# A state-space scan's start and its norm tiles: two low parts by accumulating DMA, decay sums at another place in TensorE's order, norm sums in another pool's banks

## The chip, the cores and the metric

The program runs on one core of one Trainium2 chip. The metric is the device time of one execution in microseconds (us); three executions of the kernel before took 2970.08, 2967.94 and 2969.83 us, median 2969.83. Lower is better.

## What is computed

One inference step of a two-layer streaming encoder on 1024 prompt frames and 64 frames of a running stream (1088 columns, model width 1024, fp32). Layer 0 is a Mamba-2 mixer with a SwiGLU feed-forward part, layer 1 is banded attention with a SwiGLU part; each sub-layer stands between two RMS norms. The change lies in the mixer and its scan:

```python
zxbcdt = u @ w_in                          # z, x, B, C and dt
xbc = silu(causal_conv4(xbc))              # x, B, C
dt = softplus(dt_raw + dt_bias); dA = dt * A
Acs = cumsum(dA, axis=-1)                  # within a chunk
Lm = exp(where(causal, Acs[..., :, None] - Acs[..., None, :], -inf))
CB = einsum('bcqgn,bcsgn->bcgqs', Cc, Bc)
y_diag = einsum('bcgjqs,bcsgjp->bcqgjp', CB[:, :, :, None] * Lm, xd)
chunk_states = einsum('bcsgn,bcsgjp->cbgjpn', Bc, xd * decay_to_end[..., None])
h = h * chunk_decay + chunk_states         # over chunks
y = y_diag + einsum('bcqgn,cbgjpn->bcqgjp', Cc, h_prev) * exp(Acs) + x * D
y = groupnorm(y * silu(z)) @ w_out         # RMS norm over each of 4 groups
```

## The kernel before

**Split fp32.** Every weight and activation is held as a high part h (rounded to the fp32r format) and a low part l, the rest. A product is three matmuls in one PSUM bank: h by xh (L454), h by xl (L455), l by xh (L456), over eight slices of the contraction, so a pass over one weight is 24 matmuls. `passes` (L446) issues them; after half of them and at the end it lets other work in. `Weights` loads a weight tile to a raw buffer (SP's queue, L252) and `part` (L325) splits it: ACT rounds (L340), VectorE subtracts (L341). An item that is planned with `acc` goes another way in `part`: ACT writes h (L334) and then -h in the low part's place (L335), and a DMA on POOL's queue adds the weight from memory onto it (L336). Before, only 12 parts of the feed-forward layers go that way.

**The scan's stage.** The 1088 columns are three slices (384, 384, 320), s0 to s2. First B, C and x of the first group and dt are projected slice by slice; `finish` ends that. Then the list `order` is worked off group by group; its first group is weight 1 of x and weight 0 of z, in the order x s0, x s1, z s0, z s1, z s2, x s2. An x or z pass takes one of two banks of pool pmm (tile mm) and is evicted by VectorE (L721). x goes through the convolution (L759 ACT, L761 VectorE), B and C too.

**The decay tables.** `table_task` makes dt (softplus by a polynomial, L688) and dt A (L691) on VectorE. Then on TensorE: the cumulative sums (acsp, L694), the chunk sums (lastp, L699) and the transposed table (acT, L707). ACT copies acT (row, L709), SP stores it (L710), and each `ssd_task` loads its tables MT and ea from there (L845, L848). VectorE subtracts (L854), ACT takes the exponent (L855), VectorE multiplies by CB (L878).

**A scan step** (`ssd_task`, one for each of 16 x tiles and 3 slices): transpose of x (xtp, L866), times dt (xd, L876, VectorE), times decay (xe, L877, POOL), chunk states (sp, L885), the running state (hn, L895 and L898, VectorE). For two steps at a time `ssd_out` makes yp (L816) and yo (L826), each in a bank of pool pyy, evicted by VectorE (L830, L832). The last tile of a group (every fourth) also makes the group norm's sums: `rstd` transposes them on TensorE (nst, L487), VectorE reduces (L498) and takes the root (L499 to L511); `build_y` later broadcasts the result (nbp, L517).

**PSUM.** Eight banks: pmm has 2, pax 2 (xtp, sp, bnp, cbp, acsp, lastp, nst, nbp by `ax`), pyy 4 (yp, yo, acT, and early mmp and dtp). bnp (L785) and cbp (L791) are the transpose of B and the product of C and B. A tile waits until what stood in its bank has been read.

**What sets the order.** TensorE's order is written by hand. A `Stream` keeps an estimated time, tasks are generators that yield (cost, delay, condition), and `pump` steps those that are due wherever `passes` or `unit` lets it. TB_V is the delay of `table_task` between dt A and acsp, in that estimate. The other engines' queues are put in order by a scheduler with priorities, and each works its queue in order.

Of the kernel before, what the change touches and what calls it, by code (L numbers as in the profile page):

```python
# [8 lines left out]
F32 = mybir.dt.float32  # L9
# [7 lines left out]
P = 128  # L17
# [27 lines left out]
AT_W1, AT_W2 = 6.0, 2.5  # L45
SSD_GAP, SSD_D = 4.4, 8.0
ST_W, ST_RB = (6.5, 22.0, 22.0), (6.0, 1.0, 1.0)
TB_W, TB_V = 1.0, 14.0
ES = 0.5, 0.5, 0.0
OS = 1.9, 1.4  # L50
EP_W, ER_W, EQ_W = (9.4, 9.4, 2.2), (8.9, 8.9, 3.3), (11.0, 11.0)
# [323 lines left out]
def hybrid_kernel(  # L375
# [28 lines left out]
    for _ in range(17):  # L404
# [14 lines left out]
    W = Weights(  # L419
        nc, Ring(wp, "raw", RAWB, [P, 1024]), Ring(wp, "hl", HLB, [P, 2, 1024], F32R),  # L420
        Ring(None, "half", 0, [P, 2, 512], F32R), Ring(None, "tt", 0, [P, 1024]),
    )
# [10 lines left out]
    def col(c):  # L433
        return pcs[:, c:c + 1]

    def ax(name):
        return pax.tile([P, 512], F32, tag="ax", name=name)

    def mm(name):
# [21 lines left out]
    def unit(w, u, n, evac, parts=2, pl=None):  # L461
        ps_ = mm("mm") if pl is None else pl.tile([P, 512], F32, tag="mm", name="mmx")
        passes(ps_, w, lambda k: u[k], [(k, k) for k in range(KD)], n, parts=parts)
        evac(ps_)
        st.pump()
# [16 lines left out]
    def rstd(ssum, inv, r, nb, more=None):  # L482

        sp = ax("nst")
        if more is None:
            for i in range(nb):
                PE.transpose(sp[:, i * P:(i + 1) * P], ssum[:, i * P:(i + 1) * P], ident)  # L487
        else:
            for j, t in enumerate((ssum, more)):
                for i in range(nb):  # L490
                    c = 4 * j + i
                    PE.matmul(sp[:, c:c + 1], t[:, i * P:(i + 1) * P], ones[:, 0:1], start=True, stop=True)
        with tc.high_priority(HIP):
            v = nsb.tile([P, 12], F32, tag="nv", bufs=2, name="nv")
            a, h, y = v[:, 0:nb], v[:, 4:4 + nb], v[:, 8:8 + nb]
            if more is None:
                sums = sp[:, :nb * P].rearrange("p (a b) -> p a b", b=P)
                V.tensor_reduce(a, sums, axis=mybir.AxisListType.X, op=ALU.add)  # L498
                V.tensor_scalar(a, a, inv, EPS, op0=ALU.mult, op1=ALU.add)  # L499
            else:  # L500
                V.tensor_scalar(a, sp[:, :nb], inv, EPS, op0=ALU.mult, op1=ALU.add)
                V.scalar_tensor_tensor(a, sp[:, 4:4 + nb], inv, a, op0=ALU.mult, op1=ALU.add)
            V.tensor_scalar(y.bitcast(I32), a.bitcast(I32), -0.5, float(0x5F3759DF), op0=ALU.mult, op1=ALU.add)


            V.tensor_tensor(h, y, y, op=ALU.mult)
            V.tensor_tensor(h, h, a, op=ALU.mult)
            V.scalar_tensor_tensor(a, h, RP[0], h, op0=ALU.add, op1=ALU.mult)
            V.scalar_tensor_tensor(a, a, RP[1], h, op0=ALU.add, op1=ALU.mult)
            V.scalar_tensor_tensor(a, a, RP[2], h, op0=ALU.add, op1=ALU.mult)  # L510
            V.scalar_tensor_tensor(r, a, RP[3], y, op0=ALU.add, op1=ALU.mult)  # L511

    def bcast(r, a, n, rb=None):

        bp = ax("nbp")
        for i in range((a + n + P - 1) // P):
            PE.transpose(bp[:, i * P:(i + 1) * P], r[:, i:i + 1].to_broadcast([P, P]), ident)  # L517
        if rb is None:
            rb = nsb.tile([P, 384], F32, tag="rb", bufs=1, name="rb")
        A.activation(rb[:, :n], bp[:, a:a + n], AF.Copy, scale=RL)  # L520
        return rb[:, :n]
# [35 lines left out]
    order = []  # L557
# [8 lines left out]
            else:  # L566
                order.append((("x", 15), ("z", 14), ("z", 15)))
    W.plan(*[dict(src=[w_in[t]]) for t in (32, 36, 16)])
    for grp in order:
        W.plan(*[dict(src=[w_in[{"B": 32, "C": 36, "x": 16, "z": 0}[kd_] + i]]) for kd_, i in grp])  # L570

    MGS = ((0, 1, 2), (3, 4, 5), (6, 7))
    for b in range(2):
# [30 lines left out]
    def project(qs, uq, y, src, after=None, early=None, pl=None):  # L604


        ss = {}
        for mg in MGS:
            ws = early if early and mg is MGS[0] else [W.get() for _ in mg]
            for q in qs:  # L610
                n = QS[q][1]
                st.wait_for(lambda: q in uq)
                for m, w_ in zip(mg, ws):
                    ym = y[q][m // 4][:, m % 4, :]

                    def ev(ps):
                        with tc.high_priority(HIP):
                            if src is None:
                                A.copy(ym, ps[:, :n])
                            else:  # L620
                                V.tensor_tensor(ym, src[q][m // 4][:, m % 4, :], ps[:, :n], op=ALU.add)

                    if not (ws is early and q == qs[0]):
                        unit(w_, uq[q], n, ev, pl=pl)
                    if after:
                        if m == 0:
                            ss[q] = ssum_start(n)
                        add_sq(ss[q], ym, n, m == 0)
                    if q == qs[-1]:
                        W.put()  # L630
                if mg is MGS[-1]:
                    R.put(4)
                    if src is not None and src is not y:
                        R.put(2)
                    if after:
                        after(q, ss[q])

    with ExitStack() as es:
        pyy = es.enter_context(tc.tile_pool(reuse_waits="tile", name="pyy", bufs=4, space=PSUM))
# [302 lines left out]
        def evac_of(kind, i):  # L942
            if kind == "z":
                def f(s, p_):
                    n = SL[s][1]
                    zst[i, s] = sb2.tile([P, 384], F32, tag="zs", bufs=3, name="zs")
                    scaled(zst[i, s][:, :n], p_, s, 0, n)
                    A.activation(zst[i, s][:, :n], zst[i, s][:, :n], AF.Silu)
                    if i == 15:
                        drop_u(s)  # L950
                        if s == 0:
                            st.spawn(build_y())
                return f
            if kind == "x":
                cvx = pair_t[i] = Conv(i, "xsT", 5)

                def f(s, p_):
                    cvx(s, p_)
                    st.spawn(ssd_task(i, s))
                return f  # L960
            if kind == "B":
                grp_t[i] = Conv(16 + i, "BT", 2), Conv(20 + i, "CT", 5)
                return grp_t[i][0]
            cvc = grp_t[i][1]

            def f(s, p_):
                cvc(s, p_)
                st.spawn(group_task(i, s), SSD_D)
            return f
# [71 lines left out]
        def scale_dt(s):  # L1041
            st.wait_for(lambda: s in done)
            ps = pend[s].pop(0)
            V.tensor_tensor(dtT[s][:64, :SL[s][1]], ps[:64, :SL[s][1]], rbs[s][:64, :SL[s][1]], op=ALU.mult)

        def finish(s):
            if s < 1:
                scale_dt(s)
            for e, ps in zip(ev, pend.pop(s)):
                e(s, ps)  # L1050

        for s in range(NSL):
# [23 lines left out]
                dps = dt_unit(us, n, pl, tg)  # L1076
            pend[s] = [dps] * (s < 2) + box
        finish(2)
        for grp in order:
            ws = [W.get() for _ in grp]  # L1080
            ev = [evac_of(*f) for f in grp]
            if len(grp) < 3:
                seq = [(i, s) for s in range(NSL) for i in range(len(grp))]
                if grp is order[0]:

                    seq = [(0, 0), (0, 1), (1, 0), (1, 1), (1, 2), (0, 2)]
            else:
                seq = [(0, 0), (1, 0), (0, 1), (0, 2), (2, 0), (1, 1), (2, 1), (1, 2), (2, 2)]
            for i, s in seq:
                kd_, jj_ = grp[i]  # L1090
                q = 3 * jj_ + s
                if kd_ == "x":
                    st.wait_for(lambda: so["C"] > q - 5)
                elif kd_ == "z":
                    st.wait_for(lambda: so["D"] > q - 3)
                elif kd_ == "C" and q >= 5:
                    g_, s_ = divmod(q - 5, 3)
                    st.wait_for(lambda: so["C"] > 3 * (4 * g_ + 3) + s_)
                unit(ws[i], u[s], SL[s][1], lambda p_: ev[i](s, p_))
                if s == 2:  # L1100
                    W.put()
# [5 lines left out]
            ya[q] = [v4(R.get(), QS[q][1]) for _ in range(2)]  # L1107
        project((0, 1), uy[0], ya, None)
        st.wait_for(lambda: so["D"] == 3 * XT and len(rst_done) == NG * NSL)


    class Ops:
# [428 lines left out]
    with ExitStack() as es:  # L1541
# [298 lines left out]
        for j in range(1, 8):  # L1840
# [11 lines left out]
            while left:  # L1852
# [11 lines left out]
                s, i = now  # L1864
# [135 lines left out]
```

## Time and profile before

| | us |
|---|---|
| median of three executions | 2969.83 |
| the profiled execution | 2970.8 |
| its span | 2969.1 |
| TensorE busy | 2916.9 |
| VectorE busy | 2037.2 |
| ACT busy | 1394.6 |
| POOL busy | 723.7 |

The profile is of one execution. Busy times are sums over instructions of an engine; TensorE's matmuls overlap a little, so its busy share is not a share of peak. An "idle before" in brackets on a row is the time that the engine stood still ahead of the row, with the instruction that the trace holds for its end. The scan's start, where the decay tables are made, lies at 55 to 111 us; the scan ends near 670 us. The mean granted TensorE clock was 0.996 over the span.

### The profile page before, as it was taken

What the parts mean: (1) busy time and instruction counts of PE and PEld (TensorE: products, weight loads), DVE (VectorE), ACT (ScalarE), POOL (GpSimd) and SP (SyncE); (2) the same over time, 40 slices, a digit from 0 to 9 for tenths busy, and PEclk for the clock granted to TensorE, in tenths of its full rate; (3) what the DMA queues carried; (4) which work ended last, traced back from release to release, by engine and by line L of the source; (5) the groups of instructions that cost most, each with busy time, mean ns of one, the idle gap of its engine ahead of it and who ended that gap; (6) DMA issues with size and microseconds to landing.
All of it is one profiled execution on the core that took longest, in us unless ns stands there. A gap on an engine that the chain in (4) does not pass through costs nothing.

```text
span 2969.1 us, 56218 instructions
## 1 busy us (share of the span) xinstructions
PE 2916.9 (98%) x21562; PEld 2871.9 (97%) x21562; DVE 2037.2 (69%) x4455; ACT 1394.6 (47%) x2522; POOL 723.7 (24%) x877
## 2 busy tenths in 40 slices
PE   8999999999999999999999999999999999999999
PEld 7899999999999999999999899999899999999999
DVE  7887888785768555584557878778678645475544
ACT  6564645454454222244545666556653322244443
POOL 1333333331121343451111000000131333351111
PEclk9999999999999999999999999999999999999999
DMA  3333323234564222255655322223365222245654
GB/s 123 113 106 96 104 90 110 93 118 150 172 172 129 79 76 84 73 161 175 208 175 169 96 75 78 66 67 99 110 186 171 79 79 77 78 156 171 220 174 137
DMA packets 201550, 363.35 MB, mean 122 GB/s; under 512 B 20544, under 2 KB 149280, under 8 KB 201280
## 3 DMA queue, kind: packets, MB, share of 16 engines
q1 hardware_dynamic: 199488, 353.39, 38.3%
q0 software_dynamic: 1792, 6.36, 1.1%
q8 instruction: 169, 2.77, 0.4%
q14 instruction: 101, 0.83, 0.1%
HBM read 292.47 MB, written 62.74 MB: 120 GB/s over the span
## 4 chain that ended last, share of the span: by engine, by line
PE 85%; DVE 8%; DMA 3%; ACT 2%; issue 2%; POOL 0%; SPq 0%; DVEq 0%; ACTq 0%; POOLq 0%
PE px L1280 9%; PE px L1281 9%; PE px L1282 9%; PE mm L454 7%; PE mm L456 7%; PE mm L455 7%; PE po L1480 6%; PE po L1481 6%; PE po L1479 6%; PE mmx L455 3%; PE mmx L454 3%; PE mmx L456 3%; PE ptp L1712 2%; PE po L1747 2%; PE yp L816 1%
## 5 line engine op out<-in xcount | busy, mean ns | idle before, releaser
L454 PE MATMUL mm<-r,hl 128*128 128x384 f32 (+2 forms) x1664 | 555.1, 334 | 6.1 <-ACT BT L768 3.0
L456 PE MATMUL mm<-r,hl 128*128 128x384 f32 (+2 forms) x1664 | 539.6, 324 | 3.6 <-DVE hl L353 2.9
L455 PE MATMUL mm<-r,hl 128*128 128x384 f32 (+2 forms) x1664 | 538.2, 323 | 0.0
L341 DVE TENSOR_TENSOR hl<-raw,hl 128x1024 fp32r<-128x1024 f32 (+1 forms) x219 | 257.2, 1175 | 226.8 <-ACT hl L340 220.7
L1281 PE MATMUL px<-r,hl 128*128 128x288 f32 (+1 forms) x1184 | 347.3, 293 | 0.0
L454 PEld LDWEIGHTS mm<-r,hl 128*128 128x128 f32 x1664 | 315.4, 190 | 9.0 <-ACT BT L768 3.2
L456 PEld LDWEIGHTS mm<-r,hl 128*128 128x128 f32 x1664 | 314.5, 189 | 5.7 <-DVE hl L353 4.5
L455 PEld LDWEIGHTS mm<-r,hl 128*128 128x128 f32 x1664 | 315.3, 190 | 0.3
L1280 PE MATMUL px<-r,hl 128*128 128x288 f32 x1056 | 311.0, 294 | 0.0
L1282 PE MATMUL px<-r,hl 128*128 128x288 f32 x1056 | 310.7, 294 | 0.0
L340 ACT CAST hl<-raw 128x1024 fp32r<-128x1024 f32 (+1 forms) x219 | 220.0, 1005 | 175.3 <-PE po L1481 101.6
L480 POOL TENSOR_TENSOR ssum<-ssum,sq 128x256 f32<-128x256 f32 (+3 forms) x97 | 127.8, 1318 | 637.3 <-ACT sq L479 622.0
L1281 PEld LDWEIGHTS px<-r,hl 128*128 128x128 f32 x1184 | 222.3, 188 | 0.0
L1282 PE MATMUL px<-rx,hl 128*128 128x256 f32 x768 | 214.8, 280 | 6.7 <-DVE hl L341 6.7
L1280 PE MATMUL px<-rx,hl 128*128 128x256 f32 x768 | 215.3, 280 | 0.7 <-ACT hl L340 0.7
L1480 PE MATMUL po<-rx,hl 128*128 128x384 f32 (+1 forms) x624 | 201.7, 323 | 0.1
L1280 PEld LDWEIGHTS px<-r,hl 128*128 128x128 f32 x1056 | 198.4, 188 | 0.4 <-DVE u L1295 0.3
L1282 PEld LDWEIGHTS px<-r,hl 128*128 128x128 f32 x1056 | 198.3, 188 | 0.0
L1479 PE MATMUL po<-rx,hl 128*128 128x384 f32 (+1 forms) x608 | 197.3, 324 | 0.0
L1481 PE MATMUL po<-rx,hl 128*128 128x384 f32 (+1 forms) x608 | 196.5, 323 | 0.0
L1281 PE MATMUL px<-rx,hl 128*128 128x256 f32 x640 | 178.7, 279 | 0.0
L290 POOL TENSOR_TENSOR tt<-raw 128x512 f32<-128x512 f32 x40 | 54.7, 1367 | 438.6 <-DMA raw<-in_w_f_dram 308.9
(360 smaller groups left out, 8053.6 us busy)
## 6 DMA issues: line engine op xcount, KB each, us to landing
raw<-in_w_f_dram SPq DMA_DIRECT2D x154, 512.0 KB, 3.8
rx<-in_w_f_dram SPq DMA_DIRECT2D x54, 512.0 KB, 3.6
raw<-in_w_in_dram SPq DMA_DIRECT2D x40, 512.0 KB, 3.6
MT<-ascr SPq DMA_DIRECT2D x48, 384.0 KB, 4.3
sg<-hscr SPq DMA_DIRECT2D x88, 192.0 KB, 3.5
raw<-in_w_f_dram SPq DMA_DIRECT2D x44, 384.0 KB, 3.2
raw<-in_w_so_dram SPq DMA_DIRECT2D x32, 512.0 KB, 3.8
raw<-in_w_kv_dram SPq DMA_DIRECT2D x18, 512.0 KB, 3.5
```

The source lines that it names most:

```text
L340: self.nc.scalar.copy(h, v)
L341: (eng or self.eng or self.nc.vector).tensor_tensor(lo, v, h, op=ALU.subtract)
L454: PE.matmul(ps[:, :n], h_, xh, start=(first and i == 0), stop=False)
L455: PE.matmul(ps[:, :n], h_, xl, start=False, stop=False)
L456: PE.matmul(ps[:, :n], l_, xh, start=False, stop=(last and i == nk - 1))
L480: (eng or G).tensor_tensor(ssum[:, :n], ssum[:, :n], q[:, :n], op=ALU.add)
L1280: PE.matmul(ps, wh, ah[:, k, :], start=(k == 0), stop=False)
L1281: PE.matmul(ps, wh, al[:, k, :], start=False, stop=False)
L1282: PE.matmul(ps, wl, ah[:, k, :], start=False, stop=(k == 3))
L1479: PE.matmul(ps[:, :n], wh, xh, start=(k == 0), stop=False)
L1480: PE.matmul(ps[:, :n], wh, xl, start=False, stop=False)
L1481: PE.matmul(ps[:, :n], wl, xh, start=False, stop=(k == FT - 1))
```

## The change

Three edits. The delay TB_V goes from 14 to 10. From the end of the first projections to the end of the scan, the tiles nst and nbp take a bank of pool pyy in place of one of pax. And the two weights of the first group of `order` (x 1 and z 0) are planned with `acc`, so that their low parts are made by L334 to L336.

```diff
-TB_W, TB_V = 1.0, 14.0
+TB_W, TB_V = 1.0, 10.0
...
+    side = [None]
+
     def ax(name):
+        if side[0] and name in ("nst", "nbp"):
+            return side[0].tile([P, 512], F32, tag="yy", name=name)
         return pax.tile([P, 512], F32, tag="ax", name=name)
...
-    for grp in order:
-        W.plan(*[dict(src=[w_in[{"B": 32, "C": 36, "x": 16, "z": 0}[kd_] + i]]) for kd_, i in grp])
+    for g_, grp in enumerate(order):
+        W.plan(*[dict(src=[w_in[{"B": 32, "C": 36, "x": 16, "z": 0}[kd_] + i]], acc=g_ < 1) for kd_, i in grp])
...
         finish(2)
+        side[0] = pyy
         for grp in order:
...
         project((0, 1), uy[0], ya, None)
         st.wait_for(lambda: so["D"] == 3 * XT and len(rst_done) == NG * NSL)
+        side[0] = None
```

The changed file has four lines more from `ax` on (five and six near its end), so a row's line is 4 higher there: L454 is L458, L694 is L698.

TensorE, the first group: x s0, x s1 and the start of z s0. Before (between two rows stand twelve projection matmuls of a half pass, where "..." is):

```order
L785 MATMUL bnp<-ident,BT 128x128 x3
...
L791 MATMUL cbp<-CT,BT 128x128 x3
...
L694 MATMUL acsp<-tt,U 128x288
...
L699 MATMUL lastp<-tt,ones 128x288
L707 MATMUL acT<-ident,nac 32x128 x9
L785 MATMUL bnp<-ident,BT 128x128 x3
...
L791 MATMUL cbp<-CT,BT 128x128 x3
```

and after:

```order
L698 MATMUL acsp<-tt,U 128x288
L789 MATMUL bnp<-ident,BT 128x128 x3
...
L703 MATMUL lastp<-tt,ones 128x288
L711 MATMUL acT<-ident,nac 32x128 x9
L795 MATMUL cbp<-CT,BT 128x128 x3
...
L789 MATMUL bnp<-ident,BT 128x128 x3
...
L795 MATMUL cbp<-CT,BT 128x128 x3
```

In both the first row follows the first half of x s0. acsp has moved ahead of 24 projection matmuls, bnp and cbp; lastp and acT ahead of 24 too and of cbp. Of the rest of TensorE's order only the first xtp moves: it now stands inside z s1, before it stood behind z s2. No nst or nbp moves.

VectorE, around dt A (tt from dt and negA) and the evictions of slice s2 (craw from mm; the first pair of 256 and 64 columns is C's, then comes x's). Before:

```order
L721 TENSOR_TENSOR craw<-mm,rb_145 128x256
L688 SCALAR_TENSOR_TENSOR dec<-dec,tt 128x288
L341 TENSOR_TENSOR hl<-raw,hl 128x1024
L688 SCALAR_TENSOR_TENSOR dec<-dec,tt 128x288
L721 TENSOR_TENSOR craw<-mm,rb_145 128x64
L689 SCALAR_TENSOR_TENSOR dt<-tt,dec 128x288
L721 TENSOR_TENSOR craw<-mm,rb_145 128x256
L690 MEMSET dt 64x32
L761 SCALAR_TENSOR_TENSOR CT<-craw,pcs,CT 128x323
L691 TENSOR_TENSOR tt<-dt,negA 128x288
```

and after:

```order
L725 TENSOR_TENSOR craw<-mm,rb_145 128x256
L692 SCALAR_TENSOR_TENSOR dec<-dec,tt 128x288
L725 TENSOR_TENSOR craw<-mm,rb_145 128x64
L692 SCALAR_TENSOR_TENSOR dec<-dec,tt 128x288 x2
L725 TENSOR_TENSOR craw<-mm,rb_145 128x256
L693 SCALAR_TENSOR_TENSOR dt<-tt,dec 128x288
L725 TENSOR_TENSOR craw<-mm,rb_145 128x64
L694 MEMSET dt 64x32
L695 TENSOR_TENSOR tt<-dt,negA 128x288
L341 TENSOR_TENSOR hl<-raw,hl 128x1024
L700 COPY nac<-acsp 128x288
L765 SCALAR_TENSOR_TENSOR CT<-craw,pcs,CT 128x323
```

Two splits L341 that stood ahead of these rows before are gone, and the third now stands behind dt A. C's second eviction comes with no split ahead of it, and the copy of acsp has come ahead of the convolutions of C and x.

ACT, the same stretch. Before:

```order
L340 CAST hl<-raw 128x1024
L759 ACTIVATE BT<-craw,pcs 128x323
L340 CAST hl<-raw 128x1024 x2
L767 ACT_TABLE_LOAD
L767 ACTIVATE BT<-BT 128x256
L768 ACTIVATE BT<-BT 128x64
```

and after:

```order
L334 CAST hl<-raw 128x1024
L763 ACTIVATE BT<-craw,pcs 128x323
L335 ACTIVATE hl<-hl 128x1024
L334 CAST hl<-raw 128x1024
L335 ACTIVATE hl<-hl 128x1024
L771 ACT_TABLE_LOAD
L771 ACTIVATE BT<-BT 128x256
L340 CAST hl<-raw 128x1024
L772 ACTIVATE BT<-BT 128x64
```

Two passes L335 have come in, with the convolution of B between the first weight's L334 and L335; the two DMAs L336 follow them on POOL's queue, where small copies of three columns stand before and behind.

## The prediction

> **What bounds the kernel now.** The page first, to see which engine sets the time.
>
> ```profile
> PE 2916.9 (98%) x21562; PEld 2871.9 (97%) x21562; DVE 2037.2 (69%) x4455; ACT 1394.6 (47%) x2522; POOL 723.7 (24%) x877
> ```
>
> TensorE is busy 98% of a 2969.1 us span. The change takes no matmul away, so all that it can win is TensorE's idle time, about 52 us, and time at a lowered clock. Next, the list of what TensorE waited for (total, times, longest).
>
> ```profile
> PE xtp L866 <- DVE nv L498: 4.8, 6, 0.8
> PE sp L885 <- POOL xe L877: 3.9, 1, 3.9
> PE mm L454 <- ACT BT L768: 3.0, 1, 3.0
> PE nbp L517 <- DVE nv L510: 2.4, 1, 2.4
> PE sp L885 <- DVE xd L876: 1.2, 1, 1.2
> PE sp L885 <- ACT rb L520: 0.8, 1, 0.8
> PE nbp L517 <- DVE hn L898: 0.7, 1, 0.7
> ```
>
> The second, third and fifth lie in one stage, the start of the scan, where the decay tables are made. The fourth is from the input's norm and serves below for the clock. The rest are waits for one of the two banks of pool pax, all in the scan. Of that stage, the timeline's TensorE rows (start, duration, idle time before in brackets), then rows of the other engines, with SP's queue:
>
> ```profile
> 70.74 0.41 PE L454 MATMUL mm<-r,hl 128*128 128x384 f32 x1 [2.99 <-ACT BT L768]
> 71.22 0.52 PE L456 MATMUL mm<-r,hl 128*128 128x384 f32 x1
> 74.42 0.53 PE L785 MATMUL bnp<-ident,BT 128*128 128x128 f32 x3
> 79.66 0.65 PE L694 MATMUL acsp<-tt,U 128*128 128x288 f32 x2
> 101.31 1.22 PE L885 MATMUL sp<-xe,Bn 128*128 128x128 f32 x6 [3.94 <-POOL xe L877]
> 104.39 1.62 PE L885 MATMUL sp<-xe,Bn 128*128 128x128 f32 x6 [1.21 <-DVE xd L876]
> 105.94 2.83 PE L816 MATMUL yp<-MT,xd 128*64 128x128 f32 x24
> 110.83 0.39 PE L454 MATMUL mm<-r,hl 128*128 128x320 f32 x1
> ```
>
> ```profile
> 61.49 0.66 ACT L759 ACTIVATE BT<-craw,pcs 128x323 f32<-128x323 f32 x1
> 70.38 0.22 DVE L721 TENSOR_TENSOR craw<-mm,rb 128x64 f32<-128x64 f32 x1
> 72.05 0.45 DVE L691 TENSOR_TENSOR tt<-dt,negA 128x288 f32<-128x288 f32 x1
> 73.02 0.54 DVE L761 SCALAR_TENSOR_TENSOR CT<-craw,pcs,CT 128x323 f32<-128x323 f32 x1
> 86.28 0.39 SPq L845 DMA_DIRECT2D MT<-ascr  x1
> 94.08 0.95 DVE L878 TENSOR_TENSOR MT<-MT,CB 128x768 f32<-128x768 f32 x1
> 96.22 1.27 DVE L854 TENSOR_SCALAR MT<-MT,nac 128x128 f32<-128x128 f32 x6 [1.20 <-DMA MT<-ascr]
> 99.71 1.02 DVE L876 TENSOR_TENSOR xd<-xtp,dt 128x384 f32<-128x384 f32 x2
> 104.16 0.84 DVE L898 SCALAR_TENSOR_TENSOR hn<-hn,cd,sp 128x64 f32<-128x64 f32 x4
> ```
>
> Two things are to be seen. The 2.99 us before the first x pass are put down to ACT, but that work was not an operand; VectorE's eviction at 70.38, the last of the bank that this pass writes, ended just before the matmul started, so I read it as a wait for a bank behind a busy VectorE. And the decay sums (acsp 79.66) start the table loads (86.28 the first), the third of which VectorE still waits for at 96.22, so xd (99.71) and xe are late and TensorE idles 3.94 us. So this stage is set by acsp, not by matmul work. Its gaps also cost clock (mean granted clock is the third column from the end):
>
> ```profile
> 43.00:45.00 2.00, 1.57 (x8) 1.60 (x9) 0.98 (x6) 1.02 (x3) 0.00 (x0) 0.70 0.03 8
> 71.00:73.00 2.00, 2.00 (x8) 2.00 (x8) 1.80 (x6) 0.55 (x2) 0.20 (x2) 0.52 0.89 260
> 106.00:108.00 2.00, 2.00 (x21) 2.00 (x22) 1.96 (x6) 0.00 (x0) 0.00 (x0) 0.50 0.00 0
> 243.00:245.00 2.00, 1.36 (x9) 1.39 (x10) 2.00 (x9) 0.18 (x1) 0.31 (x2) 1.00 0.69 249
> ```
>
> Half clock follows the 2.99 and the 3.94 us gaps; the first window holds the 2.4 us wait of the list and dips too; a 0.80 us gap (fourth row) does nothing.
>
> **Low parts by DMA (first x and z weight).** Out go two VectorE splits L341. In come two ACT passes L335 and two accumulating DMAs L336 on POOL's queue. The feed-forward layers already do this 12 times:
>
> ```profile
> L341 DVE TENSOR_TENSOR hl<-raw,hl 128x1024 fp32r<-128x1024 f32 (+1 forms) x219 | 257.2, 1175 | 226.8 <-ACT hl L340 220.7
> L335 ACT ACTIVATE hl<-hl x7: 1043/1046/1062, 855.4 to 2229.8; 128x1024 fp32r<-128x1024 f32 x7
> DMA to landing us min/median/max: 6.2/8.7/10.4
> ```
>
> VectorE gets 2 x 1.18 = 2.35 us, before 67.8. So the eviction of 70.38 comes before TensorE needs the bank, and that wait goes. What is late next: the first L456 needs the low part. ACT finishes L759 at 61.49 + 0.66 = 62.15, then L335 takes 1.05 us, so POOL issues at 63.2. Landing 6.2 to 10.4 us later is 69.4 to 73.6, against 71.22 when L456 ran before: -1.8 to +2.4. I take 7.5, between the fastest and the median (a choice, not a measurement): 70.7, that is -0.5. The gap stays about 2.5 us, nearest to the 2.4 one, so half clock stays as well. The z weight's DMA, some 3 us behind, is needed only after the x passes, 10 us later: nothing. POOL has only three-column copies queued behind these issues: nothing.
>
> [...]
>
> **Decay sums earlier (TB_V 14 to 10).** Nothing is added; acsp moves ahead of 24 projection matmuls, bnp and cbp, and lastp, acT, the row copies and DMAs follow. They need the table product at 72.05, itself behind three splits; with two gone and the third now behind it, about 69.2. TensorE runs the rest of x slice 0's half at half clock (71.22 to 74.42 before, 3.2 us) from 70.7 and reaches acsp at about 74.0, 5.7 us earlier than 79.66. The first table load follows, at about 80.6 instead of 86.28, and the third lands near 90.5 instead of 96.22. VectorE now stands at the copy of acsp (L696) from about 70.2 to 74.6, with the C and x convolutions queued behind it; six of them at 0.54 us (the row at 73.02) finish about 77.8, and the next consumers (cbp, then z's slice 1 through its bank) find them 0 to 1 us ahead. I cost that at 0; without that cover it is +1.
>
> At 96.0 TensorE reaches the first sp. The third table's 90.5, two groups of L854 and a z eviction put xd at 94.7 and xe at 95.8, so the 3.94 us go. What is late next is xd of the second slice: in VectorE's order it now stands behind three L878 (0.95 us, as at 94.08) and a z eviction, ending about 99.8, and the third xtp needs its bank. Then VectorE copies sp and runs four L898 (as at 104.16), 1.05 us, before the second sp can have its bank: 100.9 instead of 104.39. From there to the next projection matmul took 110.83 - 104.39 = 6.44 us at half clock, and the gap ahead (about 2.2 us) is nearest to the one that lowered it, so I keep half: 107.3. The stage gives **-3.5**. With the DMA landing at 73.6 the same chain slips by 2.9: -0.6. With full clock, yp takes the 1.53 us that it takes at 248.28 (the first row below) rather than 2.83, and sp half of its 1.62: 105.2, that is -5.6.
>
> **Norm tiles out of pool pax.** The sums (nst) and broadcasts (nbp) take one of the four banks of pyy. No row moves.
>
> ```profile
> 248.28 1.53 PE L816 MATMUL yp<-MT,xd 128*64 128x128 f32 x24
> 249.21 1.27 DVE L830 SCALAR_TENSOR_TENSOR y<-xsT,pcs,yp 128x384 f32<-128x384 f32 x2 [0.26 <-PE yp L816]
> 251.63 0.49 PE L487 MATMUL nst<-ident,ssg 128*128 128x128 f32 x3
> 661.33 0.60 DVE L830 SCALAR_TENSOR_TENSOR y<-xsT,pcs,yp 128x384 f32<-128x384 f32 x1
> 670.83 0.52 PE L487 MATMUL nst<-ident,ssg 128*128 128x128 f32 x3 [2.69 <-DVE nv L499]
> 672.15 0.69 PE L517 MATMUL nbp<-ident,rst 128*128 128x128 f32 x2 [0.80 <-DVE nv L498]
> ```
>
> Six times an xtp right behind nst waits 0.80 us for the sum's reduction: **-4.8**, since the sums no longer sit in pax. The new owner must be free: nst at 251.63 comes after the pair of L830 (done 250.48), so there a bank waits. At the end of the scan it does not: the broadcast at 660.72 now waits for L830 (661.33 + 0.60 = 661.93) and the sum behind it for the L832 that follows, about +2.0 in all. Against it stand the 0.8, 0.7 and 0.80 us waits for pax and part of the 2.69: that is 2.3 + 2.0 (I let 0.7 of the 2.69 stand, for the sum's own input), so **-2.3**; VectorE has no idle there, so 0 is possible, and -3.0 if the 2.69 goes whole. Banks: -7.1, between -4.8 and -7.8.
>
> **Sum.** -3.5 - 7.1 = -10.6 (the -0.5 is inside the stage). The profiled execution took 2970.8 us (1.7 around its span), so 2960.2; the runs' median, 2969.83, is 1.0 lower: **2959.2 us**.
>
> **Rivals.**
>
> *Slower: the norm tiles hold up the outputs.* yp and yo need all four pyy banks, and a sum keeps one until VectorE's reduction. In nine of the twelve sums outputs follow. If each held them by the 2.69 us of the worst such wait, that is +24.2; with -10.6, 2983.4. It decides from a mean of (10.6 + 5.9)/9 = 1.8 us. For it: VectorE is 69% busy and takes things in order. Against it: those reductions ended within 0.8 us of the sum.
>
> *The low part lands early.* If it takes the 3.6 us of a plain load,
>
> ```profile
> raw<-in_w_in_dram SPq DMA_DIRECT2D x40, 512.0 KB, 3.6
> ```
>
> it is there at 66.8, before L456. Then the 2.99 us and the half clock behind it (the 3.2 us from 71.22 to 74.42, at 0.52, lose 0.48 of it, 1.5) go: acsp about 4 us earlier still, the stage at -3.5 - 3.0 - 1.5 = -8.0; 2954.7. Against it: no accumulating one was under 6.2.
>
> *The stage gives its gain back.* A landing at 73.6, or VectorE saturated from 110 us on (10 of 10 us busy between 110 and 120):
>
> ```profile
> 110.00:120.00 10.00, 10.00 (x69) 10.00 (x68) 10.00 (x28) 6.30 (x10) 5.18 (x8) 1.00 0.73 215
> ```
>
> TensorE then restarts earlier only to wait for it. Left are the banks and -0.6 at most: 2962.4.
>
> *The banks bring nothing*, since each 0.8 us turns up as a wait for yp's or yo's eviction: only the stage, 2966.3.
>
> **How the numbers follow.** Forecast 0.50; slower rival 0.07; early landing 0.12; stage given back 0.18; banks for nothing 0.13. The range reaches from the full-clock and early-landing cases with the banks' best (2954.7, less 0.7 and the restart's 2.1: 2952) to the banks-for-nothing case and a little more (2967); outside stay the slower rival and the tails of the others, under 0.2. A measurement of this kernel tells 0.2%, 5.9 us, from no change: faster is below 2963.9. Forecast and early landing count nearly whole (0.60), the stage given back for two thirds (0.12): 0.72. Same 0.20: the rest of these and the banks-for-nothing case. Slower 0.08: the slower rival, and a late landing together with held-up outputs.
>
> **What would show it.** Right: no bank wait ahead of the first x pass, but a gap of about 2.5 us inside it, ahead of L456, ended by a DMA; acsp near 74; first table load near 80.6; no wait for xe at the first sp and about 2 and 1 us around the third xtp; projection matmuls again near 107; no 0.80 us waits before xtp from 240 to 560; about 1.2 us before the broadcast near 650. Wrong: the low part landing after 72 or before 68; TensorE waiting for VectorE between 107 and 130; yp waiting for a reduction; clock at 1.00 from 96 to 108.

## The result and the profile after

The changed kernel took 2950.41 us (median of four executions, 2948.38 to 2953.53) against 2969.57 for the kernel before: 19.2 us less, ratio 0.9937, 95% interval 0.992 to 0.9955. The forecast was 2959.2, its range 2952 to 2967, so the time lies 1.6 us under the range. The direction held, the size did not: nearly twice the gain that was forecast. The profiled execution took 2953.53 us, the longest of the four; its span is 2951.8, 17.3 us under that of before.

What TensorE still waited for, from the list of waits (total, times, longest), the rows that belong to the changed places:

```profile
PE nbp L521 <- DVE y L834: 3.0, 1, 3.0
PE xtp L870 <- ACT zs L952: 1.1, 1, 1.1
PE mm L460 <- DMA hl<-in_w_in_dram: 0.6, 1, 0.6
PE sp L889 <- DVE hn L902: 0.6, 1, 0.6
```

The 2.99, 3.94 and 1.21 us waits of the stage and all six of 0.80 ahead of xtp are gone. The scan's start again, rows of the timeline of TensorE, then of other engines:

```profile
68.70 0.44 PE L460 MATMUL mm<-r,hl 128*128 128x384 f32 x1 [0.61 <-DMA hl<-in_w_in_dram]
70.55 0.65 PE L698 MATMUL acsp<-tt,U 128*128 128x288 f32 x2
95.86 0.52 PE L870 MATMUL xtp<-ident,xsT 128*128 128x128 f32 x3 [1.14 <-ACT zs L952]
96.94 0.91 PE L889 MATMUL sp<-xe,Bn 128*128 128x128 f32 x6 [0.57 <-DVE hn L902]
97.78 1.53 PE L820 MATMUL yp<-MT,xd 128*64 128x128 f32 x24
101.38 0.39 PE L458 MATMUL mm<-r,hl 128*128 128x320 f32 x1
```

```profile
63.09 0.90 POOL L336 DMA_DIRECT2D hl<-in_w_in_dram  x1 [1.92 <-ACT hl L335]
77.04 0.38 SPq L849 DMA_DIRECT2D MT<-ascr  x1
95.17 0.54 DVE L880 TENSOR_TENSOR xd<-xtp,dt 128x384 f32<-128x384 f32 x1
```

The first low part was asked for at 63.09, as forecast (63.2), and landed 5.6 us later, at 68.7: before the earliest end of the range 69.4, since it was quicker than any of the twelve in the feed-forward layers of before (6.2 to 10.4). So the gap ahead of L460 is 0.61 us and not 2.5, acsp runs at 70.55 and not at 74.0, the first table load at 77.04 and not at 80.6, and projection matmuls are back at 101.38, 9.45 us earlier than 110.83 (forecast 107.3). yp takes 1.53 us and not 2.83: the clock did not fall here (1.00 in 104 to 106 us, below). (The row of the third xtp names ACT's zs; xd ended at 95.71, just ahead of it too, and in the kernels of TB_V alone and of the two edits together the same wait is put down to xd.) Windows of two stretches, of before and after (granted clock third from the end):

```profile
72.00:74.00 2.00, 2.00 (x8) 2.00 (x7) 1.56 (x5) 0.80 (x2) 0.45 (x1) 0.50 0.44 170
104.00:106.00 2.00, 1.61 (x8) 1.42 (x10) 1.00 (x5) 0.00 (x0) 0.83 (x1) 0.50 0.02 4
```

```profile
72.00:74.00 2.00, 2.00 (x13) 1.80 (x12) 2.00 (x6) 0.00 (x0) 0.00 (x0) 1.00 0.96 272
104.00:106.00 2.00, 2.00 (x14) 2.00 (x13) 2.00 (x5) 1.35 (x2) 1.30 (x2) 1.00 1.10 309
```

To see where time came from, I laid the same TensorE instructions of two traces side by side and took the difference of their start times (negative: earlier than in the kernel before; the times at the left are those of before). Each column is one profiled execution; the first two below are again the kernel before.

| us | before, 2nd | before, 3rd | after | after, 2nd | low parts | TB_V | pool | low parts + TB_V |
|---|---|---|---|---|---|---|---|---|
| 69 | -0.4 | -0.3 | 0.0 | -3.0 | +0.1 | +0.5 | -1.4 | +0.2 |
| 125 | -0.3 | +0.2 | -9.4 | -12.7 | -3.3 | -6.1 | -0.8 | -9.6 |
| 640 | -1.1 | -1.0 | -16.9 | -20.2 | -4.2 | -6.5 | -8.8 | -9.7 |
| 690 | -0.4 | -0.8 | -19.8 | -22.8 | -4.1 | -6.4 | -11.4 | -9.8 |
| 2960 | +0.3 | -0.4 | -17.3 | -22.3 | -3.6 | -4.0 | -11.2 | -7.5 |

What a stage gave is the step from one row to the next. In the changed kernel: -9.4 in the stage, -7.5 in the scan, -2.9 at its end. Afterwards 2.5 us are lost again, 2.0 of them where the clock fell for longer than in before (near 925 us: 0.50 for 6.83 us, in before for 3.41) or fell where it had not (near 1664: 0.50 for 3.41 us).

### The profile page after: what moved, and what is told of

Its sections match the earlier page's. It is cut to its first block, busy times and chain, and to the rows that moved or that the text cites. A ratio compares the mean times of both kernels' runs of the same rounds, so it can differ in the third digit from the quotient of the medians.

```text
span 2951.8 us, 56235 instructions
## 1 busy us (share of the span) xinstructions
PE 2913.9 (99%) x21562; PEld 2872.5 (97%) x21562; DVE 2031.3 (69%) x4453; ACT 1395.8 (47%) x2524; POOL 725.8 (25%) x879
## 4 chain that ended last, share of the span: by engine, by line
PE 87%; DVE 7%; DMA 3%; ACT 2%; issue 1%; POOL 0%; SPq 0%; DVEq 0%; POOLq 0%; ACTq 0%
PE px L1286 9%; PE px L1287 9%; PE px L1288 9%; PE mm L460 7%; PE mm L458 7%; PE mm L459 7%; PE po L1486 6%; PE po L1487 6%; PE po L1485 5%; PE mmx L459 3%; PE mmx L458 3%; PE mmx L460 3%; PE ptp L1718 2%; PE po L1753 2%; PE S L1687 1%
## 5 line engine op out<-in xcount | busy, mean ns | idle before, releaser
L458 PE MATMUL mm<-r,hl 128*128 128x384 f32 (+2 forms) x1664 | 554.4, 333 | 2.3 <-DVE kf L1597 0.8
L460 PE MATMUL mm<-r,hl 128*128 128x384 f32 (+2 forms) x1664 | 539.3, 324 | 4.2 <-DVE hl L353 2.9
L341 DVE TENSOR_TENSOR hl<-raw,hl 128x1024 fp32r<-128x1024 f32 (+1 forms) x217 | 255.9, 1180 | 224.4 <-ACT hl L340 221.8
L460 PEld LDWEIGHTS mm<-r,hl 128*128 128x128 f32 x1664 | 314.3, 189 | 6.2 <-DVE hl L353 4.0
L458 PEld LDWEIGHTS mm<-r,hl 128*128 128x128 f32 x1664 | 315.0, 189 | 4.4 <-DVE kf L1597 1.1
```

The lines of the kernel that those rows point to most:

```text
L341: (eng or self.eng or self.nc.vector).tensor_tensor(lo, v, h, op=ALU.subtract)
L458: PE.matmul(ps[:, :n], h_, xh, start=(first and i == 0), stop=False)
L460: PE.matmul(ps[:, :n], l_, xh, start=False, stop=(last and i == nk - 1))
```

## The experiments

Three theories are on trial. A: the stage gained more because the low part landed early and because no gap was left that lowers the clock, and the three edits add up. B: the edits work only together. C: one of them makes it all.

**One edit at a time.** Each kernel is the changed one with two of the three edits put back.

```diff
 # low parts alone
-TB_W, TB_V = 1.0, 10.0
+TB_W, TB_V = 1.0, 14.0
-        side[0] = pyy
+        side[0] = None
```

> Of the change only the two low parts by accumulating DMA. Theory A (the stage gained 9.4 us because the low part lands 5.6 us after its issue, so the 2.99 us bank wait shrinks to about 0.6 us and no half clock follows): TensorE reaches acsp about 4 us earlier (2.4 us of gap and 1.5 us of half clock), but the decay sums stand where they stood, so the wait for xe before the first sp stays at 3 to 4 us with half clock behind it; time -4 us, between -3 and -5. Rival B (the two edits only work together, the DMA alone gains nothing): within 1 us of before. Rival C (the DMA alone makes most of the stage's gain, since the tables come earlier with it): -8 us or more.

2966.4 us (11 runs), ratio 0.9989, 0.998 to 0.9998: -3.4. Its waits in the stage:

```profile
68.77 0.44 PE L460 MATMUL mm<-r,hl 128*128 128x384 f32 x1 [0.61 <-DMA hl<-in_w_in_dram]
75.77 0.65 PE L698 MATMUL acsp<-tt,U 128*128 128x288 f32 x2
97.86 0.94 PE L889 MATMUL sp<-xe,Bn 128*128 128x128 f32 x6 [4.38 <-POOL xe L881]
100.94 1.62 PE L889 MATMUL sp<-xe,Bn 128*128 128x128 f32 x6 [1.55 <-DVE xd L880]
102.49 2.83 PE L820 MATMUL yp<-MT,xd 128*64 128x128 f32 x24
```

The first gap and its half clock are gone (1.00 in 72 to 74 us), acsp comes 3.9 us earlier, and the two waits for xe and xd grow by 0.8 in all, with the half-clock yp (2.83 us, 0.50 in 102 to 104) behind them: what theory A said, but for the wait for xe, which is a little over its 3 to 4 us.

```diff
 # TB_V alone
-..., acc=g_ < 1) for kd_, i in grp])
+...) for kd_, i in grp])
-        side[0] = pyy
+        side[0] = None
```

> Of the change only TB_V 14 to 10. Theory A: the 2.99 us bank wait and the half clock from 71 to 74 us stay; acsp runs at 74.4 instead of 79.7, the tables come some 5 us earlier, the 3.94 and 1.21 us waits for xe and xd shrink to 1.5 to 2 us in all and the half clock from 102 to 108 goes: -5 us, between -3.5 and -6.5. Rival B (without the DMA, VectorE's three splits keep the table product late, TensorE waits at acsp): -2 or less. Rival C: at most -2.

2966.89 us (11 runs), ratio 0.9989, 0.998 to 0.9997: -2.9. The stage itself is worth more, -6.6 between 69 and 125 us:

```profile
71.26 0.41 PE L458 MATMUL mm<-r,hl 128*128 128x384 f32 x1 [2.99 <-ACT BT L772]
74.90 0.73 PE L698 MATMUL acsp<-tt,U 128*128 128x288 f32 x2
99.10 0.55 PE L870 MATMUL xtp<-ident,xsT 128*128 128x128 f32 x3 [0.56 <-DVE xd L880]
100.28 0.91 PE L889 MATMUL sp<-xe,Bn 128*128 128x128 f32 x6 [0.63 <-DVE hn L902]
101.11 1.53 PE L820 MATMUL yp<-MT,xd 128*64 128x128 f32 x24
```

5.15 us of waits have become 1.19 (theory A said 1.5 to 2), and with gaps this short yp runs at full clock (1.53 us, 1.00 in 102 to 104), although the 2.99 us gap stayed. TensorE did not wait at acsp, so the splits ahead of the table product do not bind (rival B falls). The median's -2.9 lies a little outside the expected -3.5 to -6.5, while the stage lies at its upper end; in the profile 2.4 us are lost again after the scan, nearly all of it where the clock fell for longer than in before, or fell where it had not, behind short gaps near 935 and 1675 us of its own time (the granted clock was 0.50 in 936 to 940 us and 0.58 in 1676 to 1680).

```diff
 # the pool alone
-TB_W, TB_V = 1.0, 10.0
+TB_W, TB_V = 1.0, 14.0
-..., acc=g_ < 1) for kd_, i in grp])
+...) for kd_, i in grp])
```

> Of the change only the norm tiles in the outputs' pool. Theory A (six stops cost 1.02 us each and not the 0.80 that the wait shows, some 0.25 us goes at the other sums, and the end of the scan gains 2.9): -10 us, between -9 and -11. The recorded prediction's price: -7.1.

2961.71 us (9 runs), ratio 0.9975, 0.9965 to 0.9985: -8.1 by the medians, under the -9 to -11 expected, and -10.5 in its profile between 125 and 690 us. Of that, 7.9 come up to 640 us and 2.6 at the end of the scan.

**Two edits together**: the change with `side[0] = None`, and nothing else put back.

> The change without the norm tiles' pool: low parts by DMA and TB_V 10 together. Theory A (the stage's two edits add up, and add to the pool's gain): the stage's offset at 125 us is -9.4 us as in the whole change, the time is 8 to 10.5 us under before and about 10 above the change. Rival (the edits alone gave -3.4 and -2.9, so -6.3): -6.3 within 1, with the missing 3 us coming only with the pool.

2962.43 us (11 runs), ratio 0.9976, 0.9967 to 0.9984: -6.8 by the medians against 2969.26. By time that is the rival's -6.3 within 1, and not theory A's 8 to 10.5, and 12.0 above the change. Where the time went, the profile decides, and there the stage is theory A's: it has -9.8 from 69 to 125 us, and the two edits alone have -3.4 and -6.6. So they add up, and the pool has no share in the stage; 2.2 us are lost again after the scan, where the clock fell for longer (near 935 us: 0.50 in 932 to 936, 0.69 in 936 to 940) or anew (near 1674: 0.57 in 1672 to 1676). The medians of most of these kernels are smaller gains than their profiles' stages (-3.4 and -2.9 alone, -6.8 together, -8.1 the pool, -19.2 all), but the intervals of each reach 2.5 us to either side or more, so they neither confirm nor refute a sum; the table above does.

**The landing, made late.** One pass of POOL over the low part ahead of its DMA:

```diff
+            if it.get("late"):
+                with self.tc.high_priority(self.pri):
+                    self.nc.gpsimd.tensor_scalar(lo, lo, 1.0, None, op0=ALU.mult)
             self.nc.gpsimd.dma_start(lo, it["src"][0], accum_op=ALU.add)
...
-..., acc=g_ < 1) for kd_, i in grp])
+..., acc=g_ < 1, late=g_ < 1) for kd_, i in grp])
```

> The whole change, with one more pass on POOL over each of the two low parts (times 1.0, in place) ahead of its DMA; nothing else. That puts the DMA 1.4 to 2.8 us later. Theory A (what the landing time decides is a gap and then the clock): TensorE's gap before the first low part grows from 0.6 us to 2 us or more, half clock follows it, and the time is 3 to 4.5 us above the change's, gap and clock together. Rival (the landing has slack or the clock stays full): above the change's by the extra gap only, 2.5 us or less, with a clock of 1.00 in 70 to 75 us.

2958.99 us (5 runs), ratio 0.9965, 0.9953 to 0.9978: 8.6 over the change's median. The pass took longer than I had put it:

```profile
60.40 3.08 POOL L338 TENSOR_SCALAR hl<-hl 128x1024 fp32r<-128x1024 f32 x1 [1.71 <-ACT hl L335]
70.42 0.69 PE L463 MATMUL mm<-r,hl 128*128 128x384 f32 x1 [5.32 <-DMA hl<-in_w_in_dram]
73.79 1.17 PE L701 MATMUL acsp<-tt,U 128*128 128x288 f32 x2
```

A gap of 5.32 instead of 0.61 us, 4.7 more; and the granted clock in 72 to 74 us was 0.50. From 66 us up to the chunk sums (lastp, at 82.2 us in before) the change gains 8.7 on before, this kernel 1.3, so 7.4 are lost: 4.7 of gap, and the other 2.7 behind it at half clock. 7.2 of the 7.4 are still there at 125 us. So the landing time had no slack here and was paid one for one, with the clock on top; theory A's place was right, its 3 to 4.5 us were too few because the pass was longer.

**The gaps kept, the clock kept up.** The kernel before, with matmuls that nobody reads in its two gaps:

```diff
+    def warm(ps, k):
+        for _ in range(k):
+            PE.matmul(ps[:, :NPC], ident, pcs[:, :NPC], start=True, stop=True)
...
+            if q == 0:
+                warm(pyy.tile([P, 512], F32, tag="yy", name="wm"), 9)
             sp = ax("sp")
...
+                if grp is order[0] and (i, s) == (0, 0):
+                    warm(pyy.tile([P, 512], F32, tag="yy", name="wm"), 7)
                 unit(ws[i], u[s], SL[s][1], lambda p_: ev[i](s, p_))
```

> The kernel before with matmuls that nobody reads (128 x 224, fp32) in its two gaps of the stage: 7 ahead of the first x pass, 9 ahead of the first sp, about 2.6 and 3.4 us of work, so that TensorE is not idle there but waits as long as before. Theory A (half of what the stage lost lies in the clock after a gap and not in the gap): the clock stays at 1.00 in 71 to 75 and in 102 to 109 us, the time falls by 2 to 4.5 us although no wait is removed. Rival (the granted clock there has another cause, or lost clock is hidden by the waits that follow): within 1 us of before, or slower.

2969.59 us (11 runs), ratio 1.0002, 0.9993 to 1.0011: no change by time, as the rival had it. Yet in its profile the clock was 1.00 in both stretches, and from 69 to 125 us it gained 3.4 us. To tell whether the half clock of before was chance, or the fill loses elsewhere, four more profiles:

> The kernel before once more, for a second profile. Theory A (a gap of 3 us or more always lowers the clock, one of 2 to 2.6 us only where it happens to fall, so the stage's 2.99 and 3.94 us gaps cost the same in every execution and the spread of the times comes from the shorter gaps at 43, 942, 1680 and 2291 us): half clock again in 71 to 75 and 102 to 109 us, another pattern at the shorter ones. Rival (the stage's half clock is itself a matter of chance, which is why filling its gaps did not move the median): clock 1.00 at one of the two places.

> The kernel before again, a third profile of it. Theory A: half clock in 71 to 75 and 102 to 109 us as in the first. Rival: clock 1.00 at one of the two places.

> The changed kernel once more. Theory A: the low part of the first x weight lands 5.3 to 6 us after its issue again, a gap under 1 us ahead of it, clock 1.00 from 66 to 110 us, the stage at -9 to -10 us against before once the difference at 60 us is taken off. Rival (5.6 us was a lucky landing): 6.5 us or more, a gap of 1.5 us or more.

> The kernel before with its two gaps of the stage filled, a second profile. Its first showed 3.4 us gained in the stage, and yet the median of its 11 runs was that of before. Theory A (the gain is real but small beside the spread from the shorter gaps): 3.4 us in the stage again, and in the rest of the program no loss that both profiles share. Rival (the fill loses elsewhere what it gains): a loss of 2 to 3 us at a place that both profiles of it show.

Before took 2971.14 and 2970.45 us, and both show 0.50 in 72 to 74 us and 0.50 in 104 to 106: all three profiles of before have the stage's half clock. The changed kernel took 2948.55 us; its low part landed 5.5 us after its issue, the gap was 1.10 (a little over the expected 1), the clock 1.00, the stage -9.7 from 69 to 125 us. The filled kernel took 2971.27 us; its stage gained 2.3 us (the clock fell once more, behind a 1.81 us wait: 0.53 in 100 to 102 us), and 6.1 us went between 480 and 1690 us: new waits of 0.64 us near 493 and 0.92 near 723, lowered clock near 668, 944 and 1681 (0.50 in 940 to 944 us and 0.57 in 1680 to 1684 of its own time). Its first profile shares a loss of 0.7 us near 720 (a new wait of 0.47) and one of 1.0 at a lowered clock near 1681, where the second profile of before has half clock as well; neither is the rival's 2 to 3 us. So both profiles have a gain in the stage, and why eleven timed runs show none of it is left open: an interval down to -2.1 us leaves room for a part of it, not for 3.4.

**Only the sums in the outputs' pool.**

```diff
-        if side[0] and name in ("nst", "nbp"):
+        if side[0] and name == "nst":
```

> The change with only the sums (nst) in the outputs' pool and the broadcasts (nbp) back in pax. Theory A (the six stops belong to the sums; the broadcast's new 3.02 us wait for L834 at the end only passes to the sum right behind it): within 1 us of the change, with a wait of 2.4 to 3 us at that nst. Rival (the broadcast's move costs these 3 us): 2 to 3.5 us under the change.

2948.43 us (5 runs), ratio 0.9934, 0.9921 to 0.9946. The end of its scan:

```profile
631.11 0.91 PE L889 MATMUL sp<-xe,Bn 128*128 128x128 f32 x6 [0.78 <-ACT rb L524]
636.93 0.40 PE L521 MATMUL nbp<-ident,rst 128*128 128x128 f32 x2 [0.72 <-DVE hn L902]
643.53 0.39 PE L521 MATMUL nbp<-ident,rst 128*128 128x128 f32 x2
644.78 0.55 PE L491 MATMUL nst<-ident,ssg 128*128 128x128 f32 x3 [0.87 <-DVE y L834]
652.57 0.55 PE L491 MATMUL nst<-ident,ssg 128*128 128x128 f32 x3 [0.96 <-DVE ssg L937]
```

By the medians that is 2.0 us under the change, more than theory A's 1 us and at the edge of the rival's 2 to 3.5; but the runs of the two kernels overlap (2947.43 to 2951.64 and 2948.38 to 2953.53), so time does not decide. The profile does for the sums: the six stops stay away, so they belong to the sums. Of the 3.02 us only 0.87 pass to the sum, less than I expected; but 0.78 and 0.72 come back as waits for pax, and 0.96 behind them. The end gives -3.4 us from 640 to 690, against -2.9 in the change: half a microsecond.

**Two of the change's remaining gaps filled** (`warm` as above: 5 in the bank of the broadcast near 43 us, 7 in a bank of pax ahead of the broadcast near 645 us).

> The change with matmuls that nobody reads in two of its remaining gaps: 5 ahead of the broadcast at 43 us (gap 2.37 us), 7 ahead of the broadcast at 645 us (gap 3.02 us). Theory A (the clock after a gap costs about as much as the fill's place saves): the clock stays at 1.00 in 44 to 48 and 645 to 649 us; 1.5 to 3 us under the change. Rival (VectorE bounds the end of the scan, so a faster TensorE there only waits): under the change by at most 1 us.

2951.39 us (5 runs), ratio 0.9942, 0.9929 to 0.9954: nothing gained. The clock was 1.00 at both places. By 62 us TensorE was 3.4 us ahead of before, as the second profile of the change was without a fill (3.0): half of that comes at the gap near 43 us, the other half near 57 us, where the second profile's clock stayed at 1.00 too (last section). At the scan's end (640 to 690 us) it gained 3.1 us against 2.9: the full clock saved 1.2 us behind the broadcast, and 1.0 of it was lost again at the last sum, in a wait of 0.77 us for VectorE (ssg), as the rival had it. No kernel here is clearly faster than the change.

## Why the forecast was half right

**What held.** The bank wait of 2.99 us went with the two splits; the next thing late was the low part, and its issue came within 0.1 us of the forecast. The decay sums moved the tables and removed the wait for xe; what came late in its place was xd of the second slice with the third xtp and VectorE's copies ahead of the second sp, as forecast. The norm's sums left pax and no output waited for them: the rival on the slower side did not come. The new wait at the broadcast near 645 us came too.

**The step that failed: the landing and the clock in the stage** (-3.5 forecast, -9.4 measured). "I take 7.5, between the fastest and the median" was the wrong choice: 5.3 to 5.9 us in the five kernels that issue it so. The forecast then kept the half clock behind the first gap, because 2.5 us was near 2.4; a gap of 2.3 to 2.4 us lowered it in eight of thirteen profiles only (last section). The low parts alone gave -3.4 where -0.5 stood. And the second gap was treated as one of 2.2 us, near enough to the one that lowered the clock; it came as 1.14 and 0.57 with work between, the clock stayed up, and TB_V alone gave -6.6 where the rest, -3.0, stood. The full-clock variant was worked out (-5.6) and so was the early landing (-8.0); both came at once. The forecast weighs them as alternatives, and only the lower end of the range adds them, to -10.1; the measured -9.4 lies inside that. So the stage made the forecast too small, but it is the banks, below, that carried the time out of the range. My 7.5 lies 1.9 us over the 5.6 measured.

**The term that was mis-sized: the banks** (-7.1 forecast, -7.8 at best; -10.4 in the profile, -7.5 up to 640 us and -2.9 after). Each 0.80 us wait cost 1.0. One of the six before, and the same sum and transpose in the changed kernel:

```profile
242.35 0.49 PE L487 MATMUL nst<-ident,ssg 128*128 128x128 f32 x3
243.64 0.52 PE L866 MATMUL xtp<-ident,xsT 128*128 128x128 f32 x3 [0.80 <-DVE nv L498]
```

```profile
232.84 0.49 PE L491 MATMUL nst<-ident,ssg 128*128 128x128 f32 x3
233.17 0.49 PE L870 MATMUL xtp<-ident,xsT 128*128 128x128 f32 x3
```

Sum to transpose took 1.29 us before (242.35 to 243.64) and takes 0.33 now, less than the 0.49 us of the sum's own row: without the wait the two overlap, and with it the overlap is lost too. The matmul behind it is 0.99 earlier; at the six places it is 0.99 or 1.02. Six times that is 6.0. Of the other 1.5, 0.8 come at the xtp near 233.6, 387.9 and 541.3 us (0.27 to 0.29 each), 0.65 near 328, where a wait of 0.38 us is gone, and 0.25 near 364; small steps the other way near 150 and 174 take some of it back. At the end, the forecast weighed waits that go against waits that come; the new one was 3.02 and not 1.2, but then 2.69 and 0.80 went whole:

```profile
644.43 0.60 DVE L834 SCALAR_TENSOR_TENSOR y<-xsT,pcs,yp 128x384 f32<-128x384 f32 x1
645.08 0.69 PE L521 MATMUL nbp<-ident,rst 128*128 128x128 f32 x2 [3.02 <-DVE y L834]
653.76 0.38 PE L521 MATMUL nbp<-ident,rst 128*128 128x128 f32 x2
```

L834 stands behind VectorE's scaling of y (L601, L603 of `build_y`), so TensorE waits for the eviction; the broadcast at 653.76 comes 18.4 us before its counterpart at 672.15, and the matmuls behind it 19.8.

**The rivals.** Of the second (the early landing) the mechanism was right: the landing took 5.6 us and not 3.6, but that was early enough. The third and fourth (the gain given back, the banks for nothing) fell: the stage's -9.4 still stood at 640 us, under the pool's.

## What to carry to other kernels

Where a transfer decides whether TensorE idles, look at the gap that it leaves for both ends of the transfer's range and price the clock at each end: with the late landing, 4.7 us of gap cost 7.4 us. A stop of TensorE can cost more than the idle time ahead of the row: 0.80 us cost 1.0 here, six times of six. When two gaps of one stage close, check whether their clock loss closes with them before keeping it in the sum, and look where the clock's changes lie in the trace: of gaps of one length, 2.3 to 2.4 us at one place, eight lowered it here and five did not.

## What the runs showed of the hardware

The accumulating DMA of 512 KB, as the first of two, landed in 5.3 to 5.9 us in the five kernels that issue it so (6.6 in the one with a POOL pass ahead), against 6.2 to 10.4 in the feed-forward layers of before. The second, issued 3 to 4 us behind it, took 7.4 us in the first profile of the change and 8.5 in the second. No run here isolates why.

A gap of 2.99 us ahead of the first x pass lowered the clock in each of the five profiles that had it: to 0.50 in 72 to 74 us in the three of before and in that of TB_V alone, to 0.58 in 70 to 72 and 0.57 in 72 to 74 in that of the pool alone. A gap of 2.3 to 2.4 us, the one near 43 us, lowered it in eight of thirteen profiles (the change with that gap filled left out) and left it in five, at 1.00 in 44 to 48 us.

What separates the two in the traces is where a gap lies. In the profile of before the granted clock falls to 0.50 at 43.78, 57.44, 71.09, 101.81, 671.84 and 941.49 us, which lie 4, 4, 9, 167 and 79 times 3.413 us apart, and it stays there for 3.41 us, after 101.81 for 6.83. In the first profile of the change it falls at 44.14, 57.79, 644.89, 921.37, 1662.06 and 2273.04 us, which lie 4, 172, 81, 217 and 179 times 3.413 us apart, and stays for 3.41, after 921.37 for 6.83. I divide both profiles into steps of this length, from 22 to 2940 us, so that the falls lie on their ends, and count TensorE's idle time in each step. Ten of the twelve falls follow a step with 1.72 to 2.99 us of it; no step at full clock that was not followed by a fall has more than 1.41. So the gap of 2.37 us near 43 us lowered the clock in before, where it lies in one step whole, and did not in the second profile of the change, where the end of a step, counted back from the fall near 919.4 us, splits it into about 0.9 and 1.4 us. Worked out from these counts (an estimate), a gap of 2.99 us that is split in its middle leaves 1.50 us in each step, between the 1.41 without a fall and the 1.72 with one; the two traces have no such case.

The other two of the twelve, at 57.44 and 57.79 us, follow a step without idle time (0.00 us). They come behind 18 small matmuls (dtn, L678, 32 columns each, at 55.03 us in before). Of seven profiles (before three times, the change twice, the filled kernel twice) all but the second of the change have a fall there, at 55.8 to 57.8 us. The first row is of before, the second of the second profile of the change, without the fall; TensorE is busy throughout in both:

```profile
56.00:60.00 4.00, 4.00 (x22) 3.96 (x22) 0.91 (x2) 1.67 (x2) 0.00 (x0) 0.68 0.00 0
56.00:60.00 4.00, 4.00 (x29) 4.00 (x28) 2.86 (x9) 2.72 (x4) 0.45 (x2) 1.00 0.15 15
```

Why they fall is open. Without the fall near 43 us, the pool alone was 1.4 us ahead of before at 69 us and the second profile of the change, where this one was missing as well, 3.0 (the table above). That is a part of the spread of some 8 us among executions of one kernel (2963.98 to 2972.62 in 21 of the kernel before).
